# Attention scores of three query blocks a head: the high-by-low product on 64 rows of TensorE, two pieces on different halves

## The chip, the core and the metric

The kernel runs on one core of one Trainium2 chip. The metric is the device time of one execution in microseconds (us). Three executions of the kernel before took 1432.52, 1433.54 and 1435.09 us; the median is 1433.54 us. A further execution was recorded by the hardware profiler; what is said of single instructions comes from that one. Engines are named as the profile names them: PE is TensorE's matrix product, PEld its weight load, DVE VectorE, ACT ScalarE, POOL GpSimd, and SP the queue that issues every DMA of this kernel.

## The reference

One layer of a trunk: an input projection, two kinds of attention side by side, gates and an output projection, a normalisation, a gated feed-forward part and a second normalisation. There are 1024 positions, a width of 1024, and 8 heads of 64 channels in each kind of attention. The change touches the two score products alone:

```python
# A: softmax over the own chunk of 64 and the 8 before it
scores = jnp.einsum('bcqhd,bckhd->bhcqk', qc, kb).astype(jnp.float32) / math.sqrt(dh)
scores = scores + bias[None, :, None, :, :]
probs = jax.nn.softmax(scores, axis=-1).astype(v.dtype)
...
# B: stick-breaking, causal, in blocks of 128 queries
z = jnp.einsum('bqhd,bshd->bhqs', q_blk, k).astype(jnp.float32) * scale
log_keep = jnp.where(causal, jax.nn.log_sigmoid(-z), 0.0)
suffix = lax.cumsum(log_keep, axis=3, reverse=True) - log_keep
w = jnp.exp(jnp.where(causal, jax.nn.log_sigmoid(z) + suffix, -jnp.inf))
```

## The kernel before

Nearly all time goes to matrix products in a 32-bit format of which TensorE keeps fewer bits. To keep accuracy, an operand is held as a high part and a low part (what the high part lost), and a product a*b is made of high*high, high*low and low*high. The big products are also cut by a scheme with seven instead of eight block products. Time runs through these stages: input projection (to about 348 us), the attention stage A (heads 0 to 7, about 348 to 464 us), the attention stage B (heads 8 to 15, which names call b0 to b7, about 464 to 641 us), then branch projections, output projection, feed-forward part.

In the attention stages a head has 64 channels, and TensorE has 128 rows. For each head, `load_qk` (L581) puts three tiles in place. `qs` holds the high part of q on partitions 0 to 63 and its low part on partitions 64 to 127. `kh` holds the high part of k twice, on both halves, and `kl` the low part of k twice. So `scores` (L603) needs two products over 128 rows: `qs` with `kh` (L608) gives high q * high k + low q * high k, and `qs` with `kl` (L609) adds high q * low k and low q * low k. Both add into one PSUM bank of the tag `sc`, of which there are two.

A head's 1024 queries are worked in 8 blocks of 128. A block's scores go against up to 640 keys (A) or up to 1024 keys (B). As a bank has 512 columns, a wide row of scores is cut in two pieces: in A blocks 0 to 3 into 320 and 320 columns, in B block 0 into 512 and 512, block 1 into 384 and 512, block 2 into 320 and 448, block 3 into 320 and 320. In `soft_block` (L630) DVE adds the bias and takes the minimum piece by piece (L641), ACT takes the exponential over the row (L646), POOL scales it (L649). In `stick_block` (L659) ACT takes two sigmoids of each piece (L674, L675), DVE runs a scan (L676), POOL multiplies (L679).

The weights are then turned by TensorE (L705), cast and split by ACT and DVE into `pt` (L111, L112), and multiplied with v (L719, L720). Between these small steps the kernel places matrix products that don't depend on the attention: gates (`gps`, L549) and, later, the branch projection of A (`yAps`, L767).

The code is written for a framework that sets all semaphores, gives out tile slots and orders each engine's instructions when the kernel is built. On the chip each engine then works through its own list in that order. A tile slot is given to its next tile when the last reader of the one before is done; a DMA that writes such a slot waits for this in the SP queue, and all DMAs behind it in that queue wait too. `load_qk` of head n+2 is called while head n is in its value products. The bias row of an A head is loaded in the same place (`braw`, L624) and turned round by ACT (`bias`, L627).

Of the kernel before, what the change touches and what calls it, by code (L numbers as in the profile page):

```python
# [11 lines left out]
F32 = mybir.dt.float32  # L12
F32R = mybir.dt.float32r
# [5 lines left out]
P = 128  # L19
# [3 lines left out]
DH = 64  # L23
# [27 lines left out]
def hybrid_trunk_kernel(ctx: ExitStack, tc, x, xt, w_in, w_v, b_gate, rel_bias, w_proj,  # L51
# [12 lines left out]
    pool = ctx.enter_context(tc.tile_pool(name="slots", bufs=1))  # L64

    def slot(tag, name, dtype=F32):
        return pool.tile([P, 1024], dtype, tag=tag, name=name, bufs=SLOTS[tag])
# [11 lines left out]
    def bank(tag, name):  # L79
        return ps.tile([P, HW], F32, tag=tag, name=name, bufs=BANKS[tag])  # L80
# [4 lines left out]
    mm = nc.tensor.matmul  # L85
    tr = nc.tensor.transpose
    dma = nc.sync.dma_start
# [191 lines left out]
    for kt in range(4):  # L279
        a, b = xraw[kt], xraw[kt + 4]  # L280
# [300 lines left out]
    def load_qk(hd):  # L581

        i, h = hd["i"], hd["h"]
        n = 2 * i + h
        q, k = (d[i][h * P:(h + 1) * P] for d in (q_dr, k_dr))
        for key, part in (("qs", None), ("kh", 0), ("kl", DH)):
            t = hd[key] = slot(key, f"{key}{n}", F32R)
            if part is None:
                dma(t.bitcast(F32), q)
            else:  # L590
                for half in (slice(0, DH), slice(DH, P)):
                    dma(t[half].bitcast(F32), k[part:part + DH])
        if hd["br"] == 0:
            hd["bias"] = rel_bias_tile(hd["n"])

# [8 lines left out]
    def scores(name, hd, b, c0, n):  # L604
        q = hd["qs"][:, b * P:(b + 1) * P]
        ksl = slice(b * P + c0, b * P + c0 + n)
        sc = bank("sc", name)
        mm(sc[:, 0:n], q, hd["kh"][:, ksl], start=True, stop=False)  # L608
        mm(sc[:, 0:n], q, hd["kl"][:, ksl], start=False, stop=True)  # L609
        return sc  # L610

    def weight_tiles(nm, g, j):

        if g == 0:
            return [slot("bw", f"w_{nm}_{j}")]
        if j % 2:
            return []
        t = slot("bw", f"w_{nm}_{j}")
        return [t[:, 0:512], t[:, 512:896]] if j == 0 else [t[:, 0:256], t[:, 256:384]]

    def rel_bias_tile(head):
        braw = slot("kp", f"braw{head}")
        src = rel_dr[head:head + 1, 0:640]
        dma(braw[:, 0:640],  # L624
            bass.AP(tensor=src.tensor, offset=src.offset, ap=[[1, P], [1, 640]]))
        bias = slot("kp", f"bias{head}")
        nc.scalar.activation(bias[:, 0:640], braw[:, 0:640][:, ::-1], AF.Copy, scale=-1.0)  # L627
        nc.gpsimd.memset(bias[0:DH, 576:640], BIG)  # L628
        nc.gpsimd.memset(bias[DH:P, 0:DH], BIG)
        return bias  # L630

    def soft_block(hd, b, s):

        nm = f"a{hd['n']}_{b}"
        bias = hd["bias"]
        w = min(5, 8 - b) * P
        st = sml.tile([P, 4], F32, name=f"st_{nm}", tag="st", bufs=8)
        cuts = [(0, 320), (320, 320)] if w == 640 else [(0, w)]
        for i, (c0, n) in enumerate(cuts):
            sc = scores(f"sc_{nm}_{i}", hd, b, c0, n)  # L640
            nc.vector.tensor_tensor_reduce(  # L641
                out=s[:, c0:c0 + n], in0=sc[:, 0:n], in1=bias[:, c0:c0 + n],
                op0=ALU.add, op1=ALU.min, scale=1.0,
                scalar=(3.0e38 if i == 0 else st[:, 0:1]), accum_out=st[:, i:i + 1])
        m = len(cuts) - 1
        nc.scalar.activation(s[:, 0:w], s[:, 0:w], AF.Exp, bias=st[:, m:m + 1],  # L646
                             scale=-1.0, accum_out=st[:, 2:3])
        nc.vector.reciprocal(st[:, 3:4], st[:, 2:3])  # L648
        nc.gpsimd.tensor_scalar(s[:, 0:w], s[:, 0:w], st[:, 3:4], 0.0, ALU.mult, ALU.add)  # L649
# [3 lines left out]
    def ident_ps():  # L653


        if not aside:
            aside.append(bank("tr", "ident_ps"))
            nc.vector.memset(aside[0], 0.0)
            nc.vector.tensor_copy(aside[0][:, 0:P], ident)  # L659
        return aside[0]  # L660

    def stick_block(hd, b, be):

        nm = f"b{hd['n']}_{b}"
        w = (8 - b) * P
        kp = slot("kp", f"kp_{nm}")
        nc.gpsimd.memset(be[:, 0:1], 0.0)
        c1 = max((4 - b) * P, 320)
        cuts = [(0, c1), (c1, w - c1)] if b < 4 else [(0, w)]
        for c0, n in cuts:  # L670
            sc = scores(f"sc_{nm}_{c0}", hd, b, c0, n)
            e = c0 + n
            m0 = max(c0, 1)
            nc.scalar.activation(kp[:, c0:e], sc[:, 0:n], AF.Sigmoid, scale=-1.0)  # L674
            nc.scalar.activation(be[:, m0:e], sc[:, m0 - c0:n], AF.Sigmoid)  # L675
            nc.vector.tensor_tensor_scan(kp[:, c0:e], kp[:, c0:e], ident_ps()[:, 0:n],  # L676
                                         kp[:, c0 - 1:c0] if c0 else 0.0,
                                         ALU.mult, ALU.bypass if c0 else ALU.add)
            nc.gpsimd.tensor_tensor(be[:, m0:e], be[:, m0:e], kp[:, m0 - 1:e - 1], ALU.mult)  # L679
# [149 lines left out]
    for hidx, hd in enumerate(heads):  # L829
        for g in range(2):  # L830
            box = []
            for j in range(4):
                def unit(hd=hd, g=g, j=j, box=box):
                    box.extend(weight_tiles(f"{'ab'[hd['br']]}{hd['n']}_{g}", g, j))
                    (soft_block, stick_block)[hd["br"]](hd, 4 * g + j, box[j])
                wunits.append(unit)
            n0 = len(PACKS[hd["br"]][0])
            for st in range(len(PACKS[hd["br"]][g])):
                vsteps.append((hd, hidx, g, st, st + g * n0, box))
# [3 lines left out]
    steps_of = {}  # L843
    goal = 0.0
    load_qk(heads[0])
    load_qk(heads[1])
    load_v(heads[0])
    for hd, hidx, g, st, pos, box in vsteps:
        nhead = len(LEAD[hd["br"]])
        if hidx < 14 and pos == nhead // 2:  # L850
            load_qk(heads[hidx + 2])
        if hidx < 15 and pos == 3:
            load_v(heads[hidx + 1])
        while wi < min(hidx * 8 + LEAD[hd["br"]][pos], len(wunits)):
            wunits[wi]()
            wi += 1
        if st == 0:
            steps_of[(hidx, g)] = value_steps(hd, g, box)
        turn, mult, begins = steps_of[(hidx, g)][st]
        turn()  # L860
        last = goal
        goal += FILL[hd["br"]] / nhead
        fill_until(0.5 * (last + goal))
        pend.append((mult, begins))
        if len(pend) > LAG:
            m_, begins = pend.pop(0)
            if begins:

                fill_until(goal)
            m_()  # L870
        fill_until(goal)
# [406 lines left out]
    for s, (p, i) in enumerate(steps[:base[4]]):  # L1278
# [28 lines left out]
        if i == NP2 - 1:  # L1307
            t0, half, first = takes[p]
# [45 lines left out]
```

## Time and profile before

| what | value |
|---|---|
| median of three executions | 1433.54 us (1432.52 to 1435.09) |
| profiled execution, its own time | 1434.07 us |
| span from its first to its last instruction | 1432.0 us |
| VectorE busy | 1021.5 us (71%) |
| ScalarE busy | 686.0 us (48%) |
| GpSimd busy | 309.4 us (22%) |
| DMA moved | 248.75 MB, 98574 packets |

A busy share says how much of the span an engine had work in flight. TensorE's instructions overlap: a product's record is longer than the distance to the next product's start, so the distance between starts is what a product costs TensorE, and the record's length is how long its result takes.

### The profile page before, as it was taken

Reading aid. Unit: us, or ns where it says so; the run is one execution under the profiler, and the core shown is the slowest. Engines: PE = TensorE matmul, PEld = TensorE weight load, DVE = VectorE, ACT = ScalarE, POOL = GpSimd, SP = SyncE. Lnnn points to the kernel's source line nnn. Section 1 sums busy time; section 2 is a strip of 40 time slices with the busy share of each in tenths; the row PEclk is TensorE's granted clock in tenths of the full one; section 3 lists DMA queues with packets and bytes.
Section 4 is the critical chain, followed back from the end, with each engine's and each line's share of the span. In section 5 each row is a group of like instructions: output and inputs, shape, how many; then the busy total and the mean of one; then the engine's idle time right before and its main releaser. Section 6 shows DMA issues by size and latency. Waiting matters only on the chain.

```text
span 1432.0 us, 18804 instructions
## 1 busy us (share of the span) xinstructions
PE 1401.2 (98%) x6592; PEld 1157.2 (81%) x6592; DVE 1021.5 (71%) x1588; ACT 686.0 (48%) x1196; POOL 309.4 (22%) x338
## 2 busy tenths in 40 slices
PE   8999999999999999999999999999999999999997
PEld 6888888888788787778887878888888888888886
DVE  8866467763878988986869996555556544875896
ACT  6444354544787889774223633333333332444540
POOL 0000000002444769661314021111111110200022
PEclk9999999999999999999999999999999999999999
DMA  7566737878875566747852143322332227853521
GB/s 250 169 179 182 236 89 272 304 265 253 209 211 167 173 182 206 216 161 285 317 214 81 67 160 105 106 96 108 111 105 84 91 97 258 318 193 104 170 81 74
DMA packets 98574, 248.75 MB, mean 174 GB/s; under 512 B 10400, under 2 KB 26784, under 8 KB 98480
## 3 DMA queue, kind: packets, MB, share of 16 engines
q1 hardware_dynamic: 98480, 247.56, 52.5%
q8 instruction: 52, 0.85, 0.2%
q14 instruction: 42, 0.34, 0.1%
HBM read 164.39 MB, written 83.13 MB: 173 GB/s over the span
## 4 chain that ended last, share of the span: by engine, by line
PE 84%; DVE 7%; ACT 3%; DMA 3%; issue 2%; POOL 0%; POOLq 0%; DVEq 0%; SPq 0%; ACTq 0%
PE sxf L178 15%; PE dn L1247 15%; PE sxp L178 9%; PE szf L178 7%; PE v L425 5%; PE ops L1106 5%; PE szp L178 5%; PE syf L178 4%; PE gps L549 3%; PE syp L178 2%; PE tp_b L705 2%; PE yAps L767 1%; DVE kp_b L676 1%; PE tp_a L705 1%; PE yBps L118 1%
## 5 line engine op out<-in xcount | busy, mean ns | idle before, releaser
L1247 PE MATMUL dn<-dr,dl 128*128 128x512 f32 x924 | 209.9, 389 | 0.0
L1247 PEld LDWEIGHTS dn<-dr,dl 128*128 128x128 f32 x924 | 173.4, 188 | 36.4 <-DVE x L1099 0.4
L679 POOL TENSOR_TENSOR w_b<-w_b,kp_b 128x511 f32<-128x511 f32 (+3 forms) x96 | 100.5, 1057 | 44.9 <-DVE kp_b L676 38.6
L676 DVE TENSOR_TENSOR_SCAN kp_b<-kp_b,ident_ps 128x512 f32<-128x512 f32 (+3 forms) x96 | 93.1, 970 | 18.1 <-ACT kp_b L674 14.2
L111 ACT CAST dl<-raw 128x512 fp32r<-128x512 f32 x77 | 47.2, 622 | 84.1 <-PE dn L1247 64.5
L1106 PE MATMUL ops<-wr,wl 128*128 128x512 f32 x336 | 78.8, 392 | 0.0
L943 POOL TENSOR_TENSOR mv<-mv,neghalf 128x1 f32<-128x1 f32 x16 | 26.9, 1682 | 236.3 <-DVE mv L942 236.3
L628 POOL MEMSET bias<- 64x64 f32 x8 | 1.2, 145 | 335.6 <-ACT bias L627 335.6
L1106 PEld LDWEIGHTS ops<-wr,wl 128*128 128x128 f32 x336 | 62.5, 188 | 12.5
L112 DVE TENSOR_TENSOR dl<-raw,dl 128x512 fp32r<-128x512 f32 x77 | 53.6, 703 | 25.9 <-ACT dl L111 25.7
L674 ACT ACTIVATE kp_b<-sc_b 128x512 f32<-128x512 f32 (+3 forms) x96 | 49.4, 514 | 19.7 <-PE sc_b L609 16.6
L1044 POOL TENSOR_TENSOR sb<-h 128x512 f32<-128x512 f32 x10 | 15.9, 1594 | 185.6 <-PE syf L178 135.5
L649 POOL TENSOR_SCALAR w_a<-w_a,st_a 128x640 f32<-128x640 f32 (+2 forms) x64 | 43.4, 684 | 56.7 <-DVE st_a L648 37.9
L178 PE MATMUL szf<-x1S63h,wcf 128*128 128x512 f32 x168 | 55.3, 390 | 0.0
L191 DVE TENSOR_TENSOR gt<-sxf,gt 128x512 f32<-128x512 f32 x21 | 14.4, 687 | 55.1 <-PE sxf L178 55.1
L112 DVE TENSOR_TENSOR pt_b<-tp_b,pt_b 128x512 fp32r<-128x512 f32 (+1 forms) x80 | 48.8, 621 | 6.9 <-ACT pt_b L111 6.7
L705 PE MATMUL tp_b<-ident,w_b 128*128 128x128 f32 x288 | 45.3, 274 | 5.0 <-DVE pt_b L112 3.2
L111 ACT CAST pt_b<-tp_b 128x512 fp32r<-128x512 f32 (+1 forms) x80 | 45.6, 572 | 9.1 <-PE tp_b L705 8.6
L675 ACT ACTIVATE w_b<-sc_b 128x511 f32<-128x511 f32 (+3 forms) x96 | 49.6, 517 | 0.0
L646 ACT ACTIVATE w_a<-w_a,st_a 128x640 f32<-128x640 f32 (+2 forms) x64 | 44.6, 697 | 8.8 <-DVE st_a L641 7.1
L1045 POOL TENSOR_TENSOR sa<-h,h 128x512 f32<-128x512 f32 x10 | 15.8, 1584 | 147.5 <-PE sxf L178 135.8
L112 DVE TENSOR_TENSOR pt_a<-tp_a,pt_a 128x512 fp32r<-128x512 f32 x64 | 41.6, 652 | 6.9 <-ACT pt_a L111 6.4
(1520 smaller groups left out, 4181.3 us busy)
## 6 DMA issues: line engine op xcount, KB each, us to landing
raw<-left_dr SPq DMA_DIRECT2D x77, 256.0 KB, 3.0
wo_dr<-wo SPq DMA_DIRECT2D x28, 512.0 KB, 4.0
wr<-wo_dr SPq DMA_DIRECT2D x28, 512.0 KB, 7.7
wLf<-in_w_ffn_in_dram SPq DMA_DIRECT2D x22, 512.0 KB, 4.4
wRf<-in_w_ffn_in_dram SPq DMA_DIRECT2D x22, 512.0 KB, 4.2
rows<-in_w_ffn_out_dram SPq DMA_DIRECT2D x22, 512.0 KB, 6.5
left_dr<-h SPq DMA_DIRECT2D x33, 256.0 KB, 2.0
v_dr<-vst SPq DMA_DIRECT2D x16, 512.0 KB, 3.0
```

The costliest lines, as they stand in the source:

```text
L111: nc.scalar.copy(dst_h, src)
L112: nc.vector.tensor_tensor(dst_l, src, dst_h.bitcast(F32), ALU.subtract)
L178: mm(acc, lw[:, ks], rx, start=(first and kt == i == 0), stop=(kt == 3 and i == 2), skip_group_check=not first)
L425: mm(banks[mt], xs[lw][:, ms], o[:, rx], start=(fresh and kt == n == 0), stop=(kt == 3 and n == 2), skip_group_check=not fresh)
L646: nc.scalar.activation(s[:, 0:w], s[:, 0:w], AF.Exp, bias=st[:, m:m + 1], scale=-1.0, accum_out=st[:, 2:3])
L674: nc.scalar.activation(kp[:, c0:e], sc[:, 0:n], AF.Sigmoid, scale=-1.0)
L675: nc.scalar.activation(be[:, m0:e], sc[:, m0 - c0:n], AF.Sigmoid)
L676: nc.vector.tensor_tensor_scan(kp[:, c0:e], kp[:, c0:e], ident_ps()[:, 0:n], kp[:, c0 - 1:c0] if c0 else 0.0, ALU.mult, ALU.bypass if c0 e ...
L679: nc.gpsimd.tensor_tensor(be[:, m0:e], be[:, m0:e], kp[:, m0 - 1:e - 1], ALU.mult)
L705: tr(tp[:, j:j + P], wt[qb - q0][:, (kb - qb) * P:(kb - qb + 1) * P], ident)
L1106: mm(acc, lw, rx, start=(fresh and n == m == 0), stop=(n == 3 and m == 2), skip_group_check=not fresh)
L1247: mm(acc, lw, rx, start=(fresh and steps[s][1] == n == 0), stop=(last and n == 2), skip_group_check=not fresh)
```

## The change

A fourth tile, `qt`, holds the columns of query blocks 0 to 2 of q with its halves swapped: the low part on partitions 0 to 63, the high part on partitions 64 to 127. It is filled by two DMAs of 64 partitions and 384 columns a head, and it has a single slot (`bufs=1`), so the tile of the next head waits for the last reader of this one.

For blocks 0, 1 and 2 of every head (always two pieces) `scores_two` issues four products: `kh` with `qs` for the first piece and `kh` with `qt` for the second, both over 128 rows; then `kl` with the high half of `qs` on rows 0 to 63 for the first piece, and `kl` with the high half of `qt` on rows 64 to 127 for the second. The term low q * low k is left out there. Blocks 3 to 7 are as before. The number of products stays as it is: 2 of 128 rows and 2 of 64 rows where there were 4 of 128.

```diff
@@ load_qk
+        qt = hd["qt"] = pool.tile([P, 3 * P], F32R, tag="qt", name=f"qt{n}", bufs=1)
+        for half in (0, DH):
+            dma(qt[half:half + DH].bitcast(F32), q[DH - half:2 * DH - half, 0:3 * P])
         if hd["br"] == 0:
             hd["bias"] = rel_bias_tile(hd["n"])
@@ after scores
+    def scores_two(name, hd, b, cuts):
+
+        q = hd["qs"][:, b * P:(b + 1) * P]
+        qt = hd["qt"][:, b * P:(b + 1) * P]
+        scs = []
+        for i, (c0, n) in enumerate(cuts):
+            sc = bank("sc", f"{name}_{i}")
+            ksl = slice(b * P + c0, b * P + c0 + n)
+            mm(sc[:, 0:n], (q, qt)[i], hd["kh"][:, ksl], start=True, stop=False)
+            scs.append((sc, n, ksl))
+        for i, (sc, n, ksl) in enumerate(scs):
+            r = slice(i * DH, (i + 1) * DH)
+            mm(sc[:, 0:n], (q, qt)[i][r], hd["kl"][r, ksl], start=False, stop=True)
+        return [sc for sc, _, _ in scs]
@@ soft_block
+        both = scores_two(f"sc_{nm}", hd, b, cuts) if b < 3 else None
         for i, (c0, n) in enumerate(cuts):
-            sc = scores(f"sc_{nm}_{i}", hd, b, c0, n)
+            sc = both[i] if both else scores(f"sc_{nm}_{i}", hd, b, c0, n)
@@ stick_block
-        for c0, n in cuts:
-            sc = scores(f"sc_{nm}_{c0}", hd, b, c0, n)
+        both = scores_two(f"sc_{nm}", hd, b, cuts) if b < 3 else None
+        for i, (c0, n) in enumerate(cuts):
+            sc = both[i] if both else scores(f"sc_{nm}_{c0}", hd, b, c0, n)
```

The order on the engines comes from the build. In the fences below L623 is the 128-row product and L627 the 64-row product of `scores_two`; before, L608 and L609 are the two of `scores`. A name such as `sc_b2_1_0` is the scores of branch b, its head 2, block 1, first piece (before, the last number but one of a B piece is its first column).

On PE, block 1 of b2 before, with the products beside it:

```order
L549 MATMUL gps14_1_4949<-xl4_291,wh_g14_4222 128x512
L608 MATMUL sc_b2_1_0_5028<-kh10_4796,qs10_4794 128x384
L609 MATMUL sc_b2_1_0_5028<-kl10_4799,qs10_4794 128x384
L608 MATMUL sc_b2_1_384_5035<-kh10_4796,qs10_4794 128x512
L609 MATMUL sc_b2_1_384_5035<-kl10_4799,qs10_4794 128x512
L705 MATMUL tp_b1_0_4_5042<-ident_69,w_b1_0_0_4705 128x128
```

The same place on PE now:

```order
L549 MATMUL gps14_1_4982<-xl4_291,wh_g14_4246 128x512
L623 MATMUL sc_b2_1_0_5061<-kh10_4826,qs10_4824 128x384
L623 MATMUL sc_b2_1_1_5063<-kh10_4826,qt10_4832 128x512
L627 MATMUL sc_b2_1_0_5061<-kl10_4829,qs10_4824 128x384
L627 MATMUL sc_b2_1_1_5063<-kl10_4829,qt10_4832 128x512
L725 MATMUL tp_b1_0_4_5075<-ident_69,w_b1_0_0_4735 128x128
```

Here the two 64-row products stand next to each other, and the neighbours are the same. So it is in 29 of the 48 rows: in 22 of the 24 of stage B and in 7 of the 24 of stage A (block 0 of every A head but a1).

On PE, block 1 of a5 before:

```order
L608 MATMUL sc_a5_1_0_3864<-kh5_3680,qs5_3678 128x320
L609 MATMUL sc_a5_1_0_3864<-kl5_3683,qs5_3678 128x320
...
L549 MATMUL gps12_0_3585<-xl7_294,wh_g12_2944 128x512
L719 MATMUL pv_a4_0_3857<-pt_a4_0_1_3824,v4_3649 128x384
L720 MATMUL pv_a4_0_3857<-pt_a4_0_1_3824,v4_3649 128x384
L608 MATMUL sc_a5_1_1_3868<-kh5_3680,qs5_3678 128x320
L609 MATMUL sc_a5_1_1_3868<-kl5_3683,qs5_3678 128x320
L719 MATMUL pv_a4_0_3857<-pt_a4_0_1_3824,v4_3649 128x128
```

And now:

```order
L623 MATMUL sc_a5_1_0_3882<-kh5_3695,qs5_3693 128x320
L627 MATMUL sc_a5_1_0_3882<-kl5_3698,qs5_3693 128x320
L740 MATMUL pv_a4_0_3875<-pt_a4_0_1_3842,v4_3664 128x384
L739 MATMUL pv_a4_0_3875<-pt_a4_0_1_3842,v4_3664 128x128
L740 MATMUL pv_a4_0_3875<-pt_a4_0_1_3842,v4_3664 128x128
L549 MATMUL gps12_0_3600<-xh7_286,wl_g12_2951 128x512
L623 MATMUL sc_a5_1_1_3884<-kh5_3695,qt5_3701 128x320
L627 MATMUL sc_a5_1_1_3884<-kl5_3698,qt5_3701 128x320
L725 MATMUL tp_a4_0_4_3937<-ident_69,w_a4_0_2_3710 128x128
```

The build has put the second piece behind other work, as before, since its bank comes free later; each 64-row product stands alone between products of 128 rows. So it is in the other 19 rows: 17 of stage A, and blocks 1 and 2 of b0.

On SP, the loads of head 4 before, and the bias load behind them:

```order
L592 DMA kh4_3460<-k_dr2_87 64x1024
L601 DMA v3_3429<-v_dr0_93 128x8x128
L589 DMA qs4_3458<-q_dr2_79 128x1024
L735 DMA y_dr0_95<-yt0_3114 128x1024
L592 DMA kh4_3460<-k_dr2_87 64x1024
L592 DMA kl4_3463<-k_dr2_87 64x1024 x2
L624 DMA braw6_3897<-rel_dr_240 128x640
```

The same place on SP now:

```order
L589 DMA qs4_3470<-q_dr2_79 128x1024
L604 DMA v3_3441<-v_dr0_93 128x8x128
L755 DMA y_dr0_95<-yt0_3123 128x1024
L592 DMA kh4_3472<-k_dr2_87 64x1024 x2
L592 DMA kl4_3475<-k_dr2_87 64x1024 x2
L595 DMA qt4_3478<-q_dr2_79 64x384 x2
L642 DMA braw5_3704<-rel_dr_240 128x640
L553 DMA g_dr11_114<-gate11_2955 128x1024
```

The two loads of `qt` stand behind those of `kl`, and the bias load that follows is that of head 5 instead of head 6; on ACT the turn of this bias row has moved accordingly, to just behind the exponential of block 5 of a3.

## The prediction
> **What bounds the kernel now.** I read the page first, then the busy time of the two attention stages, then who waits for whom there, and last the order in time of single score rows.
>
> ```profile
> span 1432.0 us, 18804 instructions
> PE 1401.2 (98%) x6592; PEld 1157.2 (81%) x6592; DVE 1021.5 (71%) x1588; ACT 686.0 (48%) x1196; POOL 309.4 (22%) x338
> PE 84%; DVE 7%; ACT 3%; DMA 3%; issue 2%; POOL 0%; POOLq 0%; DVEq 0%; SPq 0%; ACTq 0%
> ```
>
> TensorE is busy for 98% of the span, and 84% of the chain that ended last is its own work. The change touches only the attention stages, so I asked for these two stretches (columns: length, then busy time and count of PE, PEld, DVE, ACT, POOL).
>
> ```profile
> 348.00:464.30 116.30, 113.39 (x695) 95.40 (x694) 93.72 (x316) 92.10 (x211) 52.78 (x81) 1.00 0.73 200
> 464.30:641.00 176.70, 168.09 (x946) 142.06 (x946) 154.88 (x200) 146.54 (x317) 126.87 (x169) 1.00 0.62 187
> ```
>
> TensorE is idle for 2.9 us of 116.3 in A and 8.6 us of 176.7 in B, 11.5 of 293 together; the granted clock is 1.00. ACT and DVE are at 79% to 88%. So what the change gives to or takes from TensorE shows almost fully in the time; I pass on nine tenths, an estimate, since some idle time will take it up. The waits in this stretch that touch scores are small (us in total, times, longest):
>
> ```profile
> PEld sc_a L608 <- DVE st_a L641: 6.3, 20, 0.8
> PEld sc_b L608 <- ACT w_b L675: 3.9, 6, 2.0
> ACT kp_b L674 <- PE sc_b L609: 16.6, 22, 1.3
> DVE w_a L641 <- PE sc_a L609: 5.9, 9, 2.4
> ```
>
> **What one product costs.** Four score rows in order of time (start, length of the record):
>
> ```profile
> 347.95 0.30 PE L608 MATMUL sc_a<-kh,qs 128*128 128x320 f32 x1
> 348.09 0.31 PE L609 MATMUL sc_a<-kl,qs 128*128 128x320 f32 x1
> 348.24 0.31 PE L608 MATMUL sc_a<-kh,qs 128*128 128x320 f32 x1
> 348.39 0.31 PE L609 MATMUL sc_a<-kl,qs 128*128 128x320 f32 x1
> 348.53 0.39 PE L549 MATMUL gps<-xh,wh_g 128*128 128x512 f32 x1
> ...
> 483.26 0.39 PE L608 MATMUL sc_b<-kh,qs 128*128 128x512 f32 x1
> 483.48 0.39 PE L609 MATMUL sc_b<-kl,qs 128*128 128x512 f32 x1
> ...
> 487.81 0.34 PE L608 MATMUL sc_b<-kh,qs 128*128 128x384 f32 x1
> 487.99 0.34 PE L609 MATMUL sc_b<-kl,qs 128*128 128x384 f32 x1
> 488.16 0.40 PE L608 MATMUL sc_b<-kh,qs 128*128 128x512 f32 x1
> ...
> 492.05 0.31 PE L608 MATMUL sc_b<-kh,qs 128*128 128x320 f32 x1
> 492.20 0.31 PE L609 MATMUL sc_b<-kl,qs 128*128 128x320 f32 x1
> ```
>
> From start to start a product of 320 columns takes (348.53-347.95)/4 = 0.145 us, of 512 columns 0.22 us, of 384 columns (488.16-487.81)/2 = 0.175 us. Its record goes on for 0.31-0.145 = 0.165 us more, in which the next product already runs.
>
> **Gain.** Where the two 64-row products stand next to each other they use different rows and different banks, and can run at the same time; then the shorter one costs nothing. 29 rows stand so: in A 7 of 320 columns; in B 8 whose shorter piece has 512, 7 with 384 and 7 with 320. That is 7*0.145 + 8*0.22 + 7*0.175 + 7*0.145 = 1.0+1.8+1.2+1.0 = 5.0 us. The bound from the other side is nothing: no row of this trace has two products at once. I take the 5.0, because different rows and banks leave nothing shared but the weight load. In the 19 other rows a 64-row product is alone and takes as many columns as before; it gains nothing.
>
> **Price of going from 128 rows to 64 and back.** Every product and weight load in this trace reads 128*128; none shows such a change. A change of columns (512 to 320 above) costs nothing, which is the lower bound. The nearest row for the upper bounds is TensorE taking up work that it couldn't prepare:
>
> ```profile
> 349.11 0.19 PEld L608 LDWEIGHTS sc_a<-kh,qs 128*128 128x128 f32 x1 [0.39 <-DVE st_a L641]
> 349.22 0.19 PEld L609 LDWEIGHTS sc_a<-kl,qs 128*128 128x128 f32 x1
> ...
> 349.11 0.41 PE L608 MATMUL sc_a<-kh,qs 128*128 128x320 f32 x1
> 349.37 0.30 PE L609 MATMUL sc_a<-kl,qs 128*128 128x320 f32 x1
> ```
>
> Behind the wait the step is 0.26 us instead of 0.145: 0.11 us more, the distance at which weight loads follow each other (349.11, 349.22). So a start with nothing loaded ahead costs 0.11 us. If results in flight must also leave the array first, the tail of 0.165 us is added or takes its place: 0.165, or 0.275 for both. I take 0.11 us a change, by the row that is nearest: I suppose that the weights of a 64-row product can't be laid ready behind those of a 128-row product that still runs through all rows, and that the tail itself holds nothing up, as it doesn't between the products above. The other ends, 0 and 0.275, stay for the range.
>
> How many changes: a pair goes to 64 rows and back, 29*2 = 58. A lone product does so by itself, 19*2*2 = 76. Together 134, at 0.11 us 14.7 us. It is the 19 parted rows that make this costly: they pay 76 changes for nothing.
>
> The Trainium skill, page "TensorEngine Tiling (Array Packing)", section "Tiling Modes", states that changing the tiling mode, not just the tile, drains TensorE. By this rule the tail would be paid at every change: 134*0.165 = 22.1 us instead of 14.7. No run here shows a drain yet.
>
> **Other edits.** The first piece's scores are complete one product later (0.145 to 0.22 us) in the 29 pairs, the second's one earlier. ACT and DVE read the first piece first; the waits above show them waiting for scores 31 times, 22.5 us, without being the bound. Cost on the path 0, upper end 29*0.2 = 5.8 us of ACT and DVE waiting, covered by their idle 12 to 21%.
>
> The 32 `qt` loads add 16*2*98 KB = 3.1 MB to 248.75 MB, and some 0.5 us each of SP's time. They wait in SP's queue, which the rows below show around head 4 (the first product is the last of block 2 of a3, the second the first of a4; the last row is what ACT waits for bias loads in the whole run, us and times): `qt4`, behind `kl4`, waits for that last product of a3, and the bias load waits behind it.
>
> ```profile
> 392.37 1.23 SPq L592 DMA_DIRECT2D kl<-k_dr  x2
> 393.70 0.54 SPq L624 DMA_DIRECT2D braw<-rel_dr  x1
> ...
> 394.20 0.31 PE L609 MATMUL sc_a<-kl,qs 128*128 128x320 f32 x1
> ...
> DMA to landing us min/median/max: 3.9/7.1/9.6
> ...
> 401.48 0.62 ACT L646 ACTIVATE w_a<-w_a,st_a 128x384 f32<-128x384 f32 x1
> ...
> 403.35 0.31 PE L608 MATMUL sc_a<-kh,qs 128*128 128x320 f32 x1
> ...
>   DMA braw<-rel_dr: 2.8, 3
> ```
>
> `kl` is issued at 392.37, the product that frees `qt` ends at 394.5, two issues of about 0.55 us follow, so the bias load goes out at 395.7 instead of 393.70 and lands at the median 7.1 us later, 402.8. On ACT its turn now stands behind the exponential of 401.48, which is done at 402.1. ACT would wait 0.7 us there, at the extremes 0 to 3.2 us, in six heads, 0 to 19 us. ACT has 116.3-92.1 = 24 us idle in A, and its casts run ahead of TensorE by two steps. I put 1 us on the path, and keep 0 to 4. If that cover is gone, the casts of `pt` come late and TensorE's value products wait. `qt` itself is issued some 8 us before its head's first row (a4 starts at 403.35, the load is out at 395.6); I count 0.
>
> **Sum.** (14.7 - 5.0)*0.9 + 1 = 9.7 us on the profiled execution's 1434.07: 1443.8. That execution is 0.5 us above the median of the runs shown (1433.54), so 1443 us for the median.
>
> **Rivals.**
> 1. The changes cost nothing and the pairs run side by side: **faster**. For it: different columns follow each other free of charge in the rows above. Against: two half loads must come ahead of a pair, at 0.11 us each, against a step of 0.145 in which they hide. Time: -5.0*0.9 + 1 = -3.5, at best -5.0: 1428.5 to 1430.
> 2. The change doesn't do what it says: 64-row products run one after the other like any others, without a price. TensorE's time stays, the bias loads remain: 0 to +2, 1433.5 to 1435.5.
> 3. The change of shape costs the tail or tail and load, 0.165 to 0.275 us, over 134 changes 22.1 to 36.9 us: (22.1-5.0)*0.9+1 = 16.4 to (36.9-5.0)*0.9+4 = 32.7, 1450 to 1466. For it: a half product can't follow into rows that the wave of a whole one still crosses. The Trainium skill's rule on changing the tiling mode, page "TensorEngine Tiling (Array Packing)", would come to this. Against: the record's tail also holds the way of the result into the bank, which need not hold up the next product.
>
> The price decides the sign: at 5.0/134 = 0.037 us a change gain and price are equal. A lone product of 64 rows would be right either way in its length, so only its neighbours' steps tell.
>
> Of rival 1 the Trainium skill, page "TensorE: Matmul & The Clock Gate", section "Part 3: Packing small matmuls — row/col tiling", says that products on different row groups run at the same time, about 4 ns apart. By it a pair would gain all but 29*0.004 = 0.1 us of the 5.0. It speaks of packed products alone, not of going in and out between whole ones; no run here shows it so far.
>
> **How the numbers follow.** Forecast, a price of 0.06 to 0.165 us a change: 0.40; its own range 1437 to 1450 (0.06: (8.0-5.0)*0.9+1 = 3.7). Rival 3: 0.12. Rival 1: 0.26. Rival 2: 0.16. A price under 0.06 that gain and bias loads nearly cancel: 0.06. The range goes from rival 1 in full, 1428.5, into rival 3, 1460. A measurement of this kernel can tell about 0.2% (2.9 us) from no change: below 1430.7 is faster, above 1436.4 slower. Rival 1 lies on that edge: 0.17 of its 0.26 is faster. Faster 0.19 with what else may come out well; same 0.27 (rest of rival 1, most of rival 2, the small price); slower 0.54.
>
> **What would show it.** The price: steps around a lone L627 in A, before it and behind it, longer than 0.145 by 0.11 each; near 0 is rival 1 or 2, 0.165 or more rival 3. The gain: two L627 of a pair starting within a few hundredths of each other; a full step apart is rival 2. The bias loads: ACT waiting for `braw` by more than 2.8 us in all. By stage: A has 7*2+17*4 = 82 changes, B 22*2+2*4 = 52, so A is longer by (9.0-1.0)*0.9+1 = 8.2 us, B by (5.7-4.0)*0.9 = 1.5, and all behind 641 us keeps its length. Wrong would I be above all if starts of neighbours of lone 64-row products keep their 0.145 us; then the whole 14.7 us falls away.

## The result and the profile after

| kernel | median | ratio to before, 95% interval |
|---|---|---|
| before (4 executions beside the change) | 1433.03 us | 1 |
| after (4 executions) | 1447.56 us (1444.72 to 1448.78) | 1.0097 [1.0081, 1.0112] |

The change costs 14.5 us. The profiled execution of after took 1446.88 us, 12.8 us more than that of before. From the page of after, the span, the busy times, and the shares of the chain that ended last:

```profile
span 1444.9 us, 18849 instructions
...
PE 1417.1 (98%) x6592; PEld 1154.1 (80%) x6592; DVE 1024.8 (71%) x1588; ACT 686.6 (48%) x1196; POOL 307.1 (21%) x338
...
PE 87%; DVE 6%; ACT 3%; issue 2%; DMA 1%; POOL 0%; POOLq 0%; DVEq 0%; SPq 0%; ACTq 0%
```

TensorE has as many products as before and 15.9 us more of busy time; the other engines hardly moved. The two attention stages, A from its first score to the first of B, B from there to its last score (length, then busy time and count of PE, PEld, DVE, ACT, POOL, then granted clock, DMA share and GB/s):

```profile
347.80:473.70 125.90, 124.06 (x695) 95.97 (x694) 96.17 (x317) 92.66 (x212) 52.66 (x81) 1.00 0.70 197
473.70:654.00 180.30, 173.70 (x943) 137.99 (x942) 155.12 (x199) 145.54 (x316) 125.27 (x168) 0.99 0.62 190
```

A is 9.6 us longer and B 3.6 us. What lies behind B has kept its length (1444.9-654.0 = 790.9 us, before 791.0). TensorE is idle for even less: 1.8 us in A, 6.6 in B.

What the new products do is seen in single rows. A lone 64-row product in A, between a whole score product and a transpose, on PE and then on PEld:

```profile
427.95 0.30 PE L623 MATMUL sc_a<-kh,qt 128*128 128x320 f32 x1
428.19 0.41 PE L627 MATMUL sc_a<-kl,qt 64*128 64x320 f32 x1
428.53 0.44 PE L725 MATMUL tp_a<-ident,w_a 128*128 128x128 f32 x2
...
428.19 0.18 PEld L627 LDWEIGHTS sc_a<-kl,qt 64*128 64x128 f32 x1 [0.28 <-issue]
428.52 0.20 PEld L725 LDWEIGHTS tp_a<-ident,w_a 128*128 128x128 f32 x2 [0.16 <-issue]
```

Of 320 columns a step was 0.145 us. Now the step before the 64-row product is 428.19-427.95 = 0.24, and the step behind it 0.34. The two weight loads in question start with their products instead of ahead of them. A pair in B, of 512 and 512 columns:

```profile
492.51 0.39 PE L623 MATMUL sc_b<-kh,qs 128*128 128x512 f32 x1
492.73 0.39 PE L623 MATMUL sc_b<-kh,qt 128*128 128x512 f32 x1
493.05 0.50 PE L627 MATMUL sc_b<-kl,qs 64*128 64x512 f32 x1
493.05 0.50 PE L627 MATMUL sc_b<-kl,qt 64*128 64x512 f32 x1
493.48 0.66 PE L725 MATMUL tp_b<-ident,w_b 128*128 128x128 f32 x4
...
493.05 0.18 PEld L627 LDWEIGHTS sc_b<-kl,qs 64*128 64x128 f32 x1 [0.35 <-issue]
493.05 0.18 PEld L627 LDWEIGHTS sc_b<-kl,qt 64*128 64x128 f32 x1
493.48 0.42 PEld L725 LDWEIGHTS tp_b<-ident,w_b 128*128 128x128 f32 x4 [0.24 <-issue]
```

The two products start together (3 to 4 ns apart in the trace), and so do their loads: the pair does what it says. But the step into it is 0.32 and the step out of it 0.43, where 0.22 is usual. So the visit costs 0.10+0.21 us and, as the experiments show, another 0.11 us at the next whole product (about 0.06 where transposes follow, as here); it gains one step of 0.22. From the waits of the whole run (us in total, times, longest):

```profile
PEld sc_a L627 <- issue: 8.7, 41, 0.3
PEld sc_b L627 <- issue: 7.7, 26, 0.4
ACT kp_b L694 <- PE sc_b L627: 16.3, 16, 1.9
ACT kp_b L694 <- PE sc_b L612: 6.7, 12, 0.8
DVE w_a L660 <- PE sc_a L627: 6.2, 10, 2.8
ACT bias L645 <- DMA braw<-rel_dr: 1.5, 1, 1.5
```

The first two rows count the visits to 64 rows: 41 in A and 26 in B, each a weight load that waits for nothing the profile can name. They are new. ACT now waits for scores of B for 16.3+6.7 = 23.0 us (L612 is the second product of the blocks left as they were), where it was 16.6; DVE waits for those of A about as long as before, and ACT waits less for the bias loads.

### The profile page after: what moved, and what is told of

The parts are those of the page before. It is cut to its first block, busy times and chain, and to the rows that moved or that the text cites. A ratio compares the mean times of both kernels' runs of the same rounds, so it can differ in the third digit from the quotient of the medians.

```text
span 1444.9 us, 18849 instructions
## 1 busy us (share of the span) xinstructions
PE 1417.1 (98%) x6592; PEld 1154.1 (80%) x6592; DVE 1024.8 (71%) x1588; ACT 686.6 (48%) x1196; POOL 307.1 (21%) x338
## 4 chain that ended last, share of the span: by engine, by line
PE 87%; DVE 6%; ACT 3%; issue 2%; DMA 1%; POOL 0%; POOLq 0%; DVEq 0%; SPq 0%; ACTq 0%
PE sxf L178 15%; PE dn L1267 14%; PE sxp L178 9%; PE szf L178 7%; PE v L425 5%; PE ops L1126 5%; PE szp L178 5%; PE syf L178 4%; PE gps L549 4%; PE syp L178 2%; PE tp_b L725 2%; PE yAps L787 2%; PE plainf L1052 1%; PE tp_a L725 1%; DVE kp_b L696 1%
## 5 line engine op out<-in xcount | busy, mean ns | idle before, releaser
L694 ACT ACTIVATE kp_b<-sc_b 128x512 f32<-128x512 f32 (+3 forms) x96 | 49.1, 511 | 26.6 <-PE sc_b L627 16.3
L1065 POOL TENSOR_TENSOR sa<-h,h 128x512 f32<-128x512 f32 x10 | 15.9, 1588 | 147.2 <-PE sxf L178 120.8
```

## The experiments

Two measures are used below. Stage A is counted from the first score product of A to the first of B, stage B from there to the first product of B's branch projection (`yBps`). And every TensorE step in them is set against its length where nothing is waited for (0.145 us at 320 columns, 0.227 at 512, 0.108 for a transpose); "beyond" is what the two stages have above the sum of these, with a pair counted once, by its longer piece.

| kernel | ratio | A us | B us | visits A, B | beyond, us |
|---|---|---|---|---|---|
| before | 1 | 116.5 | 192.6 | 0, 0 | 26.5 |
| after | 1.0097 [1.0081, 1.0112] | 126.0 | 196.8 | 41, 26 | 45.2 |
| whole | 1.0023 [1.0013, 1.0034] | 118.4 | 194.1 | 0, 0 | 29.9 |
| pairs | 1.0026 [1.0016, 1.0036] | 117.1 | 197.0 | 9, 26 | 36.5 |
| lone | 1.0142 [1.0127, 1.0158] | 126.9 | 203.3 | 48, 48 | 47.5 |
| three | 1.0075 [1.0057, 1.0093] | 120.6 | 198.8 | 9, 26 | 40.0 |
| order_only | 1.0040 [1.0027, 1.0053] | 118.3 | 196.9 | 0, 0 | 32.5 |
| loads_only | 0.9995 [0.9984, 1.0006] | 116.9 | 190.5 | 0, 0 | 24.8 |

The granted clock is not the same in these profiles. In stage B, after and lone have one stretch of 3.4 us at half the clock, pairs has two, and order_only one of 6.8 us; three has one of 3.4 us in stage A; before, whole and loads_only have none there (see the last section). A stretch of 3.4 us can add up to 1.7 us to its stage and to the last column.

The theory (A) was that the changes of rows cost the time; its rivals, that the order of the four products or the added loads do, or that the price is that of each 64-row product and not of the visit.

### whole: all rows back, order and loads kept

```diff
-            r = slice(i * DH, (i + 1) * DH)
-            mm(sc[:, 0:n], (q, qt)[i][r], hd["kl"][r, ksl], start=False, stop=True)
+            mm(sc[:, 0:n], (q, qt)[i], hd["kl"][:, ksl], start=False, stop=True)
```

> All of the change but the 64-row shape: the qt loads, the swapped halves and the order high, high, low, low stay; the two products with kl take all 128 rows. Theory A (TensorE pays for going to 64 rows and back, and the rest is near nothing): the median of before within 2 us, 1432 to 1436, and steps of 0.145 and 0.227 us around the scores. Theory B (the qt loads hold up SP and with it the bias loads, or the later first piece holds up ACT and DVE): most of the 14.5 us stays, 1440 or more, with ACT waiting for braw.

Measured: 1437.3 us (10 executions) beside 1434.14 (19). So 11.3 of the 14.5 us are the 64-row shape, price and gain together, and 3.2 are not. Theory A alone would have left at most 2: something else in the change costs as well, and the runs order_only and loads_only below separate it.

### pairs: only the rows in which the two pieces stand side by side

```diff
@@ soft_block
-        both = scores_two(f"sc_{nm}", hd, b, cuts) if b < 3 else None
+        both = scores_two(f"sc_{nm}", hd, b, cuts) if b == 0 else None
```

> 64 rows only where the two products stand together: block 0 in A, blocks 0 to 2 in B (low q times low k is left out there); blocks 1 and 2 of A are as before. Some 31 visits to 64 rows instead of 67. Theory A with the price read from the changed kernel's trace, 0.09 going in, 0.20 going out and 0.05 for the next product, 0.34 us a visit: 8*(0.34-0.145) + 8*(3*0.34-0.227-0.175-0.145) = 1.6+3.8 = 5.4 us on TensorE, 4 to 5 of it in the time: 1437 to 1438.5, still slower. By the prediction's price (0.22 a visit): 8*0.075+8*0.11 = 1.5 us, 1434.5. Theory C (only the lone products cost, pairs gain): 1430 or less.

Measured: 1438.79 us (10 executions). Without the lone visits of A, A is back to 117.1 us. B, with all its pairs, is longer than before and than in whole. But up to 3.4 us of it are the two stretches at half the clock; without them it would have about 193.6 us, where whole has 194.1, and the ratio's interval overlaps that of whole. So this run excludes that pairs gain much (1430 us or less was theory C), and does not tell whether a pair pays for its own visit. The run dn_two below does.

### lone: no pairs and no qt, each low product on rows 0 to 63 alone

```diff
@@ scores
-        mm(sc[:, 0:n], q, hd["kl"][:, ksl], start=False, stop=True)
+        r = slice(0, DH if b < 3 else P)
+        mm(sc[:, 0:n], q[r], hd["kl"][r, ksl], start=False, stop=True)
```

Here the order is that of before, and there are 96 lone visits.

> The kernel before, with the product of q and kl of blocks 0 to 2 on rows 0 to 63 alone, in both pieces (low q times low k is left out there): no qt, no loads, no pairs, 96 visits to 64 rows. Theory A: 96 visits at 0.34 to 0.40 us are 33 to 38 us on TensorE, with 0.8 passed on 26 to 31 us: 1459 to 1464. By the prediction's 0.22 a visit: 21*0.9 = 19 us, 1452. Theory B: there are no loads of qt, so the time of before, 1433.

Measured: 1454.7 us, 20.6 us more than before, between the two forecasts. The steps read 0.34 to 0.40 us more for a visit, some 0.37 in the middle, so TensorE's work grew by 96*0.37 = 35.5 us, and the time by 0.58 of that. Where the rest went is in the stages (same columns as above):

```profile
348.00:474.90 126.90, 126.43 (x695) 97.39 (x694) 95.04 (x317) 91.98 (x212) 52.83 (x81) 1.00 0.66 183
474.90:661.80 186.90, 184.36 (x943) 142.11 (x942) 157.03 (x200) 147.31 (x316) 125.93 (x168) 0.99 0.59 176
```

TensorE's idle time fell from 2.9 to 0.5 us in A and from 8.6 to 2.5 us in B. That is 8.5 us. The table's last column gives more: 47.5-35.5 = 12.0 us beyond, where before had 26.5. A wait shorter than the overlap of two records (0.165 us) never shows as idle time, but it shows in the distance between starts.

### three: all three terms of these rows on 64 rows, as three pairs

```diff
+        for j, (key, swap) in enumerate((("kh", 0), ("kh", 1), ("kl", 0))):
+            for i, (sc, n, ksl) in enumerate(scs):
+                r = slice(i * DH, (i + 1) * DH)
+                mm(sc[:, 0:n], (q, qt)[i ^ swap][r], hd[key][r, ksl],
+                   start=(j == 0), stop=(j == 2))
```

> As the run pairs, but in its rows all three terms (high*high, low*high, high*low) are pairs of 64-row products, so that one visit holds three pair steps instead of one and no 128-row product. Theory A1 (the price is paid once a visit): three steps as before, only 16 rows with unequal pieces have 256 columns more, 16*0.11 = 1.7 us: 1 to 2 us above the run pairs. Theory A2 (every 64-row product pays for its own unhidden weight load, 0.11 us): two more steps with 0.11 in 32 rows, 7 us above the run pairs.

Measured: 1445.48 us, 6.7 us more than pairs: by the time alone the price would be that of every product. The rows say otherwise. One visit on PE, three pairs of 384 and 512 columns between a gate product and four transposes:

```profile
492.42 0.40 PE L549 MATMUL gps<-xh,wl_g 128*128 128x512 f32 x1
492.75 0.44 PE L627 MATMUL sc_b<-kh,qs 64*128 64x384 f32 x1
492.75 0.62 PE L627 MATMUL sc_b<-kh,qt 64*128 64x512 f32 x2
493.09 0.39 PE L627 MATMUL sc_b<-kh,qs 64*128 64x512 f32 x1
493.21 0.33 PE L627 MATMUL sc_b<-kl,qs 64*128 64x384 f32 x1
493.32 0.39 PE L627 MATMUL sc_b<-kl,qt 64*128 64x512 f32 x1
493.64 0.66 PE L726 MATMUL tp_b<-ident,w_b 128*128 128x128 f32 x4
```

The steps of the longer piece are 0.33 going in, 0.34 for the first pair, 0.23 for the second, 0.32 for the third: within a visit the second and third pair pay nothing. The time went into waits of TensorE: over 0.7 us long it has 15 in these stages, 13.9 us in all above the usual step, where pairs has 5 with 6.1. Six are in A at a score product. These two groups of waits were 7.2 and 4.8 us in pairs:

```profile
PEld sc_a L611 <- DVE st_a L661: 8.5, 18, 1.4
...
PEld tp_b L726 <- DVE pt_b L112: 7.1, 11, 2.9
```

So the forecast "A2" met the number for another reason. In the two profiled executions the stages A and B together are 319.4 us long in three and 314.1 in pairs, 5.3 us apart. Of this 1.8 us are the products' own lengths, as A1 had it, and 3.5 stand in the last column of the table; the two groups of waits above make 3.6. What the medians differ by beyond that is not traced to a place.

### dn_lone, dn_two, dn_four, dn_whole: the price by itself

The last big stage (`dn`) has 924 products of 512 columns one behind the other, and TensorE hardly waits there. Its first 66 steps have 12 products each, in threes of high*high, high*low and low*high. The third product of some threes is put on 64 rows, so that half of its sum is left out: one of four threes in dn_lone, a neighbouring pair in dn_two, four as two pairs in dn_four. dn_whole has the order of dn_four with 128 rows.

```diff
@@ triple
-            mm(acc, lw, rx, ...
+            rs = rows if n == 2 else slice(0, P)
+            mm(acc, lw[rs], rx[rs], ...
@@ the loop, dn_four
+            triple(sets[p][mt], s, mt, i == NP2 - 1, (0, 1))
+        for mt in range(4):
+            triple(sets[p][mt], s, mt, i == NP2 - 1, (2,), (slice(0, DH), slice(DH, P))[mt % 2])
```

> The price by itself, in the last stage (dn, L1247), where TensorE has no wait: in each of its first 66 steps one product of 128x512 (low by high, first bank) takes rows 0 to 63 alone, so half of its sum is left out; nothing else changes. 66 visits. Theory A with the price that the changed kernel shows between products of 512 columns, 0.092 in, 0.203 out and 0.11 at the next whole product, 0.405 us: 26.7 us, 1460. By the prediction's 0.11 a change, 0.22 a visit: 14.5 us, 1447.5. If a change costs nothing here: 1433.

> As dn_lone, but the low by high products of two banks stand together, one on rows 0 to 63, the other on rows 64 to 127 (half of each sum is left out): 66 visits with one pair each. Theory A: 66*(0.405-0.227) = 11.7 us, 1445. If the two don't run at the same time: 26.7 us or more, 1460. By the prediction's price: 66*(0.22-0.227) = -0.5 us, 1432.5.

> As dn_two with the low by high products of all four banks together: 66 visits with two pairs each (half of each sum is left out). Theory A1 (a price once a visit): 66*(0.405-2*0.227) = -3.2 us, 1430: the point at which a visit pays for itself is passed. Theory A2 (every 64-row product pays for an unhidden weight load): 66*(0.405+0.11-0.454) = +4 us, 1437.

> The order of the run dn_four (two products a bank, then the third of all four banks), with all products on 128 rows. In dn_four the trace has whole products at 0.231 us from start to start instead of 0.227. If that comes from the order: 66*12*0.004 = 3 us above before, and dn_four's visits with two pairs have then saved about that much. If it comes from the visits: the time of before, and a visit with two pairs is worth nothing.

Measured, the length from the first to the last start of these 792 products:

| kernel | 792 products, us | a visit | ratio |
|---|---|---|---|
| before | 179.29 | | 1 |
| dn_lone | 205.69 | (205.69-179.29)/66 = +0.400 | 1.0180 [1.0160, 1.0199] |
| dn_two | 192.71 | +0.203 | 1.0086 [1.0063, 1.0109] |
| dn_four | 178.18 | -0.017 | 1.0001 [0.9989, 1.0014] |
| dn_whole | 179.29 | 0 | 1.0004 [0.9995, 1.0012] |

Here nothing else waits, and the price passes into the time in full: 66*0.400 = 26.4 us, and dn_lone took 27.1 us longer (1459.75 beside 1432.68). A pair doesn't pay for its own visit: dn_two is 0.203 us a visit above before. One visit of dn_lone on PEld, then the groups of its 64-row instructions over the whole run (busy us, mean ns, idle us before them and why):

```profile
1238.38 0.41 PEld L1249 LDWEIGHTS dn<-dr,dl 128*128 128x128 f32 x2
1239.14 0.18 PEld L1249 LDWEIGHTS dn<-dr,dl 64*128 64x128 f32 x1 [0.35 <-issue]
1239.57 0.30 PEld L1249 LDWEIGHTS dn<-dr,dl 128*128 128x128 f32 x2 [0.25 <-issue]
...
L1249 PE MATMUL dn<-dr,dl 64*128 64x512 f32 x66 | 32.9, 498 | 0.0
L1249 PEld LDWEIGHTS dn<-dr,dl 64*128 64x128 f32 x66 | 12.1, 183 | 23.2 <-issue 23.2
```

PEld stands still for 0.35 us before the 64-row load, and 0.25 us before the next load of 128 rows; elsewhere it loads ahead. The 64-row record is 498 ns, 0.11 us longer than the 389 ns of a whole product. In the trace the starts of this visit are 0.319, 0.428 and 0.333 us apart instead of 0.227. All three fit one reading: at each change the product before has to run out (0.092 us), and then the weights are loaded in the open (0.107 us). Going in is 0.227+0.092; the 64-row product is 0.107+0.227+0.092; the next whole one 0.107+0.227. Twice 0.199 is 0.398, beside the 0.400 of the table.

The Trainium skill, page "TensorEngine Tiling (Array Packing)", section "Tiling Modes", says that a change of the tiling mode drains TensorE. The rows agree: the run-out of 0.092 us is there at every change, both ways, beside the open load.

One visit of dn_four on PEld:

```profile
1223.03 0.19 PEld L1249 LDWEIGHTS dn<-dr,dl 128*128 128x128 f32 x1
1223.58 0.30 PEld L1249 LDWEIGHTS dn<-dr,dl 64*128 64x128 f32 x4 [0.36 <-issue]
1224.24 0.76 PEld L1249 LDWEIGHTS dn<-dr,dl 128*128 128x128 f32 x4 [0.36 <-issue]
```

Four loads of 64 rows follow one another without a pause, the second pair's under the first pair's products. A visit with two pairs of 512 columns gains 2*0.227 = 0.454 for 0.400, and about breaks even. It gains less than the difference because its whole products are 0.231 us apart instead of 0.227. In dn_whole they stay at 0.227, so this too comes with the visits; why is open.

### order_only and loads_only: the two other parts

```diff
@@ order_only: no loads, qs for both pieces, 128 rows
+        qt = q
+            mm(sc[:, 0:n], (q, qt)[i], hd["kl"][:, ksl], start=False, stop=True)
@@ loads_only: qt is loaded and used, each piece's two products together, 128 rows
             mm(sc[:, 0:n], (q, qt)[i], hd["kh"][:, ksl], start=True, stop=False)
+            mm(sc[:, 0:n], (q, qt)[i], hd["kl"][:, ksl], start=False, stop=True)
```

> The run whole was 0.23% above before with no 64-row product. Here only its order high, high, low, low stays: both pieces use qs on all 128 rows, and there is no qt and no load of it. Theory D (the order costs: the second high product needs the second bank early, and the first piece is done one product later): 2 to 4 us above before. Theory E (the qt loads cost): within 1 us of before.

> The other half of the run whole: the qt loads stay and the second piece is computed with qt, but on all 128 rows and in the order of before (high, low, high, low). Theory D: within 1 us of before. Theory E: 2 to 4 us above before, with waits on SP or on what stands behind qt there.

Measured: 1439.49 us (8 executions) and 1431.65 us (12), beside 1433.32 (25). The loads cost nothing. Writing the four products as high, high, low, low costs 5.7 us by itself, somewhat above the forecast, where the run whole has 3.2 for order and loads together; the two intervals overlap. Part of the 5.7 goes with the clock: the 8 executions have a mean granted clock of 0.9965, the 25 beside them 0.9976, and 0.0011*1433 = 1.6 us. Stage A is 1.8 to 1.9 us longer than before in both runs. TensorE's idle time there before score products, until DVE has read the bank, is 0.4 us before, 1.6 in order_only and 2.2 in whole. In B the same waits, for ACT, did not grow in order_only (2.2 us before, 0.9 there).

What the order does is seen at block 1 of a B head, on PE in order_only (L620 is the high and L623 the low product), then on DVE and ACT:

```profile
553.53 0.34 PE L620 MATMUL sc_b<-kh,qs 128*128 128x384 f32 x1
554.10 0.50 PE L620 MATMUL sc_b<-kh,qs 128*128 128x512 f32 x1 [0.23 <-ACT w_b L691]
554.44 0.57 PE L623 MATMUL sc_b<-kl,qs 128*128 128x384 f32 x2
558.78 1.08 PE L721 MATMUL tp_b<-ident,w_b 128*128 128x128 f32 x4 [3.77 <-DVE pt_b L112]
...
550.84 4.32 DVE L749 TENSOR_TENSOR yt<-yt 64x1024 f32<-64x1024 f32 x1
555.80 0.55 ACT L690 ACTIVATE kp_b<-sc_b 128x384 f32<-128x384 f32 x1
557.98 1.26 DVE L112 TENSOR_TENSOR pt_b<-tp_b,pt_b 128x512 fp32r<-128x512 f32 x2
```

The second piece's high product waits for its bank, which ACT still reads. The low product of the first piece has a bank and stands behind it: it starts at 554.44, where it could have followed at 553.53+0.175 = 553.70. So it starts 0.74 us later than it could. The turn of the weights behind it then waits 3.77 us, and the longest such wait of PE before was 1.8. The late piece is not what holds it up: ACT has no idle time between 551.99 and 557.71 us and reads the piece at 555.80, 1.0 us after it is complete (554.78). What ends the wait is the split of `pt` on DVE at 557.98. DVE has no idle time from 550.84 to 560.09, and its addition at 550.84 took 4.32 us; at the six other heads it takes 1.22 to 1.24, at this head 1.88 in before and 2.18 in whole. Why it took so long is open, and so is whether the order brings it about. How the order comes to cost 3 to 6 us is therefore seen in the waits in A alone; the rest is open.

## Why the prediction came out as it did

The forecast was 1443 us, range 1428.5 to 1460; it is 1447.6. Sign and main mechanism were right, the sum was 9.7 us where 14.5 were measured, and the terms were off in both directions.

- **What bounds the stages**: TensorE, as said. In lone its idle time is down to 3.0 us of 313.8.
- **Gain of the pairs, 5.0 us**: right. The two products of a pair start 3 to 4 ns apart. The Trainium skill, page "TensorE: Matmul & The Clock Gate", section "Part 3: Packing small matmuls — row/col tiling", gives about 4 ns, and the rows agree.
- **Price of a change, 0.11 us: this is the term that was mis-sized.** It is 0.20 us (0.400 for a visit). "I suppose that the weights of a 64-row product can't be laid ready" was right, at 0.107 us. "The tail itself holds nothing up" was wrong: 0.092 us of run-out come on top at every change. Rival 3 had the kind, "tail and load", but with 0.165 us for the tail; the part of a record that must run out before the next shape starts is shorter than what it overlaps with its like. By the prediction's own sign (0.165 or more is rival 3) the price is rival 3's, which was given 0.12, and not the forecast's 0.06 to 0.165; the time stayed in the forecast's own range because less of the price was passed on. On TensorE the 67 visits cost 44*0.35+23*0.40 = 24.6 us instead of 14.7 (0.35 where transposes follow, 0.40 elsewhere).
- **Passing on nine tenths**: too much. The shape's 11.3 us (after less whole) over 24.6-5.0 = 19.6 us on TensorE is 0.58; lone gives 0.58 too. The step that failed is reading slack from idle time: 11.5 us were idle by records, but 26.5 us lay beyond the steps' own lengths, and of this about 15 were used up in lone. In the `dn` stage, where there is no such slack, all of the price passed on.
- **First piece later, 0 us**: wrong, though within the upper end of 5.8 that was given. Order and loads cost 3.2 us (whole) and the order alone 5.7 (order_only), of which 1.6 go with the clock. The prediction looked at ACT and DVE waiting for the piece, and not at TensorE waiting for the second bank, with a product that has a free bank queued behind. Those waits of TensorE grew in A, by 1.2 to 1.8 us; where the rest arises is open.
- **Bias and qt loads, +1 us**: 0 (loads_only 0.9995 [0.9984, 1.0006]). The landing was taken at the median of before, 7.1 us; in after it is 4.3, and ACT's waits for it fell from 2.8 to 1.5 us.
- **By stage**: A +8.2 was forecast and +9.6 came, B +1.5 and +3.6 (up to 1.7 of it the clock), the rest unchanged, as it is.

In sum: 19.6 us on TensorE instead of 9.7, times 0.58 instead of 0.9, is 11.3 instead of 8.7; the order adds 3.2, and the loads 0 instead of 1. Two errors of opposite sign, price and share, hid each other: that the forecast came as near as it did is partly luck.

No version faster than before was found. In the scores a visit has one pair, which gains 0.227 us at most and costs 0.400. Two pairs of 512 columns a visit, each in the place of two whole products, would be needed to break even. The three pairs of the run three do not give that: they stand in the place of four whole products, so they too gain a single step.

## What to carry to other kernels

Price a change of TensorE's rows by the visit, both ways, and ask how many columns run side by side within one: here 0.40 us against 0.227 us a full pair. Take an engine's slack from the distances between starts and not from its idle time, since overlapping records hide short waits. When the order of products into two banks changes, look at which product now stands ready behind one whose bank isn't free; here one such product started 0.74 us late, though what that cost is not shown.

## What the hardware showed that was not expected

Both ways of a change cost alike, 0.092 us of run-out and 0.107 us of load. And the price of a visit is nearly the same for one product (0.400 us), a pair (0.203+0.227 = 0.430) and two pairs (2*0.227-0.017 = 0.437). The 0.03 us between them is about what the whole products lose by standing a little further apart.

The granted clock sagged for short stretches. From the windows of 20 us, first after, then order_only (two rows), with the clock in the third column from the end:

```profile
580.00:600.00 20.00, 17.97 (x92) 14.21 (x91) 16.97 (x21) 12.82 (x29) 10.93 (x16) 0.91 0.58 172
```

```profile
540.00:560.00 20.00, 16.00 (x87) 13.22 (x86) 16.77 (x18) 16.39 (x33) 17.64 (x16) 0.94 0.61 175
560.00:580.00 20.00, 19.89 (x102) 16.67 (x101) 15.12 (x21) 15.27 (x33) 14.86 (x22) 0.89 0.54 164
```

At 0.91 a window loses 20*0.09 = 1.8 us of TensorE's speed; in order_only the two lose 1.2+2.2 = 3.4 us, which is about what its stage B has above that of whole (196.9 against 194.1). In after the stretch follows a wait of TensorE of 2.5 us, from start to start; in order_only it begins inside one of 4.2 us. But whole has a wait of 2.6 us in the same place and kept 1.00, and lone sagged to 0.91 after 1.6 us, so a long wait alone isn't the rule.

The clock records of the traces say more. Each sag is a stretch at half the clock, 3.41 us long (6.83 in order_only), and it starts a whole number of 3.413 us steps behind the first clock record of its trace: (592.22-11.95)/3.413 = 170 in after, (557.54-11.41)/3.413 = 160 in order_only. In the step ahead of it TensorE was busy for 0.9 to 2.3 us. So it matters where a wait falls among these steps. The run dn_whole has the attention stages of before; its wait of 2.2 us at 575.9 lies inside one step, 574.9 to 578.3, and a sag follows. In before the same wait, at 577.3, lies across the end of a step at 578.7, and the clock stays at 1.00; so does the wait of whole, across 582.4. Even this isn't the whole rule: before had TensorE busy for only 1.7 us of the step from 544.6 and kept 1.00. What sets a sag off stays open in part, and with it some 2 us of the order's cost.
